# One token block goes ahead of the others, and two of four blocks take their experts by gathered rows

## The chip, the cores and the metric

The kernel runs on one core of one Trainium2 chip. A core has five engines that run at the same time, each through its own instructions in order: TensorE (PE, with its weight loads shown as PEld), VectorE (DVE), ScalarE (ACT), GpSimd (POOL) and SyncE (SP, which here only issues DMAs). Sixteen DMA engines move data between the device memory and the on-chip memory. The metric is the device time of one execution in microseconds.

## The reference, cut to what matters

512 tokens of width 2048 pass one layer. Everything is float32.

```python
def reference(...):                     # x is (1, 512, 2048)
    xn = rms_norm(h, attn_norm_gain)
    proj = xn @ w_in                    # q, k, v of 16 "fox" heads and 16 dilated heads, and forget gates
    fox_o = forgetting_attention(...)   # causal softmax attention, bias: cumulative sum of log forget gates
    dil_o = dilated_attention(...)      # causal, three (window, dilation) patterns, partial rotary
    h = h + concat(rms_norm(fox_o), rms_norm(dil_o)) @ w_out
    hn = rms_norm(h, ffn_norm_gain)
    h = h + peer(hn, ...)
    return rms_norm(h, final_norm_gain)

def peer(x, w_query, sub_keys, expert_down, expert_up):   # 16384 experts of one neuron
    q = x @ w_query                                       # 8 heads, two halves of 128
    scores = einsum('thpc,hpnc->thpn', q, sub_keys)       # 128 keys per half
    vals, idx = top_k(scores, 16)
    # the 16 largest of the 256 sums of one value of each half -> 16 experts per head, 128 per token
    hdn = gelu(einsum('ted,td->te', expert_down[experts], x))
    return einsum('te,ted->td', softmax_gates * hdn, expert_up[experts])
```

Attention is causal: a token needs the keys and values of itself and of earlier tokens only.

## The kernel before, in words

Tokens are four blocks of 128. A product of float32 numbers is made of three matmuls (`mm3`, L87 to L91): each operand is split into a high and a low part of type float32r, and high by high, high by low and low by high are summed in PSUM. A weight arrives in pieces of 128 x 1024 (512 KB). `load_split` (L75) has SP fetch the piece to `raw` (three buffers), ACT round it to `hi` (L83, two buffers) and DVE, or POOL where the caller says so, subtract to `lo` (L84, two buffers).

**Trunk.** All 512 tokens run together. The attention norm makes `xn`; `pv` makes the values (4 column groups, 8 pieces each; the weights are the moving operand, 512 columns, and one matmul serves one token block). Attention goes through 16 pairs of heads: `project` makes q and k of a pair (2 products of 2 pieces, 24 matmuls a piece, the weights stationary and all 512 tokens moving), the dilated pairs turn part of q and k by small DMAs (`rt<-xr`), and `head` makes row maxima, a transposed row of them that a DMA writes below q, weights, exponentials and the output (`o_d`, `o_f`). The tiles `qk` that hold a head's q and k have three buffers. Then come the output projection (`po`, 32 pieces), the ffn norm (`ht`), and routing: the queries (`pq`, 32 pieces, 512 tokens moving), scores, the 16 largest by DVE, and one-hot products that pick the expert numbers (L522 to L525, some on POOL).

**Dense part.** For token blocks 0 to 2 (`ND` = 384 tokens) all 16384 experts are computed and those not chosen get a gate of zero. 128 expert tiles of 128 experts: `down_tile` makes hidden values (48 matmuls, 384 tokens moving), the gates come from a table `g_d` in device memory that one-hot products fill before (L586 to L599, 12 chunks of 32 tokens, `gm`), and 32 groups of `NG` = 4 tiles are summed in PSUM per chunk of the output (`up`) and added to `yacc` on chip (L723). Ten expert tiles (`HOLD`) are computed ahead of their gates.

**Gathered block.** For block 3 (`GB`) only the chosen experts are fetched: `gather_step` (L612) issues one indirect DMA on POOL that brings one expert row of 8 KB for each of the 128 tokens (`rows`, three buffers, 1 MB), and DVE multiplies it with the token (down rows, L624) or adds it weighted (up rows, L632). 128 steps for down and 128 for up are spread over the dense part; each may start only after a named matmul of it.

**What sets the order.** The program is written straight through; a scheduler turns it into one order per engine, by place in the program and by what is ready. A tile's buffer is taken again only when its last reader is done. Each engine, and SP's queue of DMA issues too, keeps its order: an instruction that waits holds up all behind it.

Of the kernel before, what the change touches and what calls it, by code (L numbers as in the profile page):

```python
# [43 lines left out]
# pairs (i, j) of ranks that can be among the 16 largest sums, in flat order  # L44
# [5 lines left out]
def peer_block(ctx, tc, x, x_t, w_qk, w_v, w_fg, w_o, w_pq, sub_keys, down_t, down, up_t, up,  # L50
               gains, fox_bias, ffn_row, fin_row, cos_t, sin_t, dil_mask, fox_mask, out, dbg=None):
    nc = tc.nc
    dbg = dbg or {}
# [9 lines left out]
    gn = const.tile([P, 3 * NK], F32, name="gn")      # attn | fox, dil | ffn gains by feature  # L63
# [4 lines left out]
    ahead = []  # L68

    def fetch(src, pool):  # L70
        raw = pool.tile([P, 1024], F32, tag="raw", name="raw", bufs=3)
        DMA.dma_start(raw, src)
        return raw

    def load_split(src, lo_on=None, pool=None, bufs=2):  # L75
        """One piece [128, 1024] of a weight, as two float32r parts that sum to it exactly."""
        pool = pool or wts
        raw = ahead.pop(0) if ahead else fetch(src, pool)
        if isinstance(raw, tuple):
            return raw  # L80
# [12 lines left out]
    def rstd_of(ss, n, name, width=NB):  # L93
        """(ss / n + eps) ^ -1/2"""
# [11 lines left out]
    # ---------------------------------------------------------------- attention norm  # L106
    act = tc.tile_pool(name="act", bufs=1)
    act_p = act.__enter__()
    xn = [act_p.tile([P, NK, S], F32R, name=f"xn{i}") for i in range(2)]

    def split_gain(dst, k, ps, gain):
        """dst[:, k, :] (hi, lo) = gain * ps"""
        A.activation(dst[0][:, k, :], ps, AF.Copy, scale=gain)
        V.scalar_tensor_tensor(dst[1][:, k, :], ps, gain, dst[0][:, k, :].bitcast(F32), ALU.mult, ALU.subtract)

# [5 lines left out]

    wf = wts.tile([P, NK, NH], F32, tag="raw", name="wf", bufs=3)
    DMA.dma_start(wf, w_fg)
# [6 lines left out]
    with tc.tile_pool(name="xin", bufs=1, side="right") as xp:  # L130
        ones = xp.tile([P, P], F32, name="ones")
        G.memset(ones, 1.0)
        rps = bank("s", "rps")
        for t in range(NB):
            xx = xp.tile([P, D], F32, tag="x", name=f"x{t}", bufs=4)
            DMA.dma_start(xx, x[t * P:(t + 1) * P])
            junk = xp.tile([P, D], F32, name="junk", bufs=1)
            ss = xp.tile([P, 1], F32, name=f"ss{t}")
            A.activation(junk, xx, AF.Square, accum_out=ss)
            dg = diag_of(rstd_of(ss, D, f"x{t}", 1), 0, f"x{t}")  # L140
            PE.matmul(rps[:, t * P:(t + 1) * P], ones, dg, start=True, stop=True)     # rstd along the rows
        xt = []
        for q in range(4):
            xx = xp.tile([P, 4, S], F32, name=f"xt{q}")
            DMA.dma_start(xx, x_t[:, q * 4:(q + 1) * 4])
            xt.append(xx)
            if q < 2:
                ahead.append(fetch(w_v[0, q], wts))
        rb = xp.tile([P, S], F32, name="rb")
        A.copy(rb, rps)  # L150
        ahead.append(load_split(None))
        ahead.insert(0, ahead.pop())
        for k in range(NK):
            xx = xt[k // 4][:, k % 4]
            (G if k % 2 else V).tensor_tensor(xx, xx, rb, ALU.mult)
            A.activation(xn[0][:, k], xx, AF.Copy, scale=gn[:, k:k + 1])
            V.scalar_tensor_tensor(xn[1][:, k], xx, gn[:, k:k + 1], xn[0][:, k].bitcast(F32), ALU.mult, ALU.subtract)
# [4 lines left out]
    mixed = mix_p.tile([P, NB, D], F32, name="mixed")  # L162
    aug_d = dram.tile([NH, 6, 2, S], F32, name="aug_d")
    with tc.tile_pool(name="heads", bufs=1, side="right") as hp_:
# [645 lines left out]
```

## Time and profile before

| | |
|---|---|
| three runs | 3514.08, 3514.9 (median), 3518.09 us |
| profiled execution, its own time from the first to the last instruction (span) | 3513.9 us |
| PE, PEld busy | 3387.2 us (96%), 3143.6 us (89%) |
| DVE, ACT, POOL busy | 2403.6 us (68%), 1192.2 us (34%), 604.7 us (17%) |
| moved by DMA | 708.31 MB, mean 202 GB/s |

A matmul's busy time is modelled and overlaps that of the next, so PE's busy share says that it is occupied, not how fast. What a matmul costs in a stream is the length of a stretch divided by the number of matmuls in it. The profiled execution has no other time of its own than its span; it lies 1.0 us under the median of the runs.

### The profile page before, as it was taken

The numbers are of one execution on the slowest core, as the hardware profiler recorded it, in microseconds if no ns is written. First come the engines' busy times: TensorE is split into PE (matmuls) and PEld (weight loads), VectorE is DVE, ScalarE is ACT, GpSimd is POOL, SyncE is SP. The second block draws the span as 40 slices with busy tenths as digits, with TensorE's granted clock in tenths as the row PEclk, the third lists the DMA queues.
The fourth block names the chain that finished last, engine by engine and source line by source line (L and its number), as shares of the span: only waits on it lengthen the run. The fifth ranks groups of instructions, "written<-read, shape, count | busy, mean of one in ns | idle before, by whom it ended". The sixth has DMA issues, their size and how long they took to land.

```text
span 3513.9 us, 46718 instructions
## 1 busy us (share of the span) xinstructions
PE 3387.2 (96%) x18385; PEld 3143.6 (89%) x18385; DVE 2403.6 (68%) x3673; ACT 1192.2 (34%) x1655; POOL 604.7 (17%) x386
## 2 busy tenths in 40 slices
PE   6999999999998877999999999999999999999997
PEld 4887788878877766999999999999999999999997
DVE  5236654453489999677777777677777777777755
ACT  3224443342322277332323232333233232333233
POOL 2000000000154365221111211111111111111100
PEclk9999999999999899999999999999999999999999
DMA  4232222224432134877777777777777777777753
GB/s 180 90 98 65 71 76 63 74 88 141 155 97 78 37 138 166 319 277 272 282 279 280 269 281 285 279 268 283 283 279 277 274 277 288 271 273 283 289 170 108
DMA packets 197244, 708.31 MB, mean 202 GB/s; under 512 B 17888, under 2 KB 67424, under 8 KB 161184
## 3 DMA queue, kind: packets, MB, share of 16 engines
q1 hardware_dynamic: 159312, 435.43, 37.1%
q0 software_dynamic: 36864, 268.45, 19.4%
q8 instruction: 144, 2.36, 0.3%
q10 hardware_dynamic: 848, 1.44, 0.1%
q14 instruction: 76, 0.62, 0.1%
HBM read 669.08 MB, written 35.00 MB: 200 GB/s over the span
## 4 chain that ended last, share of the span: by engine, by line
PE 85%; DVE 10%; issue 2%; POOL 2%; DMA 1%; ACT 1%; ACTq 0%; SPq 0%; POOLq 0%; DVEq 0%
PE up L89 10%; PE up L91 10%; PE up L90 10%; PE dn L90 10%; PE dn L91 10%; PE dn L89 10%; PE mm L91 3%; PE mm L90 3%; PE mm L89 3%; PE po L89 2%; PE po L90 2%; PE po L91 2%; PE pv L90 1%; PE pv L91 1%; PE pv L89 1%
## 5 line engine op out<-in xcount | busy, mean ns | idle before, releaser
L83 ACT ACTIVATE hi<-raw 128x1024 fp32r<-128x1024 f32 x416 | 439.5, 1057 | 803.8 <-PE dn L91 356.8
L89 PE MATMUL dn<-hn,lo 128*128 128x384 f32 x2048 | 695.8, 340 | 4.0 <-POOL lo L84 4.0
L90 PE MATMUL dn<-hn,hi 128*128 128x384 f32 x2048 | 695.9, 340 | 0.0
L91 PE MATMUL dn<-hn,hi 128*128 128x384 f32 x2048 | 695.8, 340 | 0.0
L89 PE MATMUL up<-hn,ulo 128*128 128x384 f32 x2048 | 688.7, 336 | 3.1 <-DVE ulo L713 2.7
L91 PE MATMUL up<-hn,uhi 128*128 128x384 f32 x2048 | 688.1, 336 | 0.0
L90 PE MATMUL up<-hn,uhi 128*128 128x384 f32 x2048 | 688.1, 336 | 0.0
L84 DVE TENSOR_TENSOR lo<-raw,hi 128x1024 fp32r<-128x1024 f32 x366 | 447.8, 1224 | 282.6 <-ACT hi L83 282.3
L712 ACT ACTIVATE uhi<-uraw 128x1024 fp32r<-128x1024 f32 x256 | 271.7, 1062 | 631.9 <-PE up L91 615.8
L632 DVE SCALAR_TENSOR_TENSOR yg<-rows,coef,yg 128x2048 f32<-128x2048 f32 x127 | 298.5, 2350 | 224.4 <-DMA rows<-in_up,gidx 224.4
L624 DVE SCALAR_TENSOR_TENSOR rows<-rows,hng 128x2048 f32<-128x2048 f32 x128 | 293.2, 2290 | 223.2 <-DMA rows<-in_down,gidx 223.1
L89 PEld LDWEIGHTS dn<-hn,lo 128*128 128x128 f32 x2048 | 386.1, 189 | 5.2 <-POOL lo L84 4.3
L89 PEld LDWEIGHTS up<-hn,ulo 128*128 128x128 f32 x2048 | 385.0, 188 | 4.3 <-PE up L91 3.6
L91 PEld LDWEIGHTS dn<-hn,hi 128*128 128x128 f32 x2048 | 386.0, 188 | 0.4
L90 PEld LDWEIGHTS dn<-hn,hi 128*128 128x128 f32 x2048 | 385.7, 188 | 0.5
L90 PEld LDWEIGHTS up<-hn,uhi 128*128 128x128 f32 x2048 | 385.0, 188 | 0.0
L91 PEld LDWEIGHTS up<-hn,uhi 128*128 128x128 f32 x2048 | 385.0, 188 | 0.0
L713 DVE TENSOR_TENSOR ulo<-uraw,uhi 128x1024 fp32r<-128x1024 f32 x256 | 312.1, 1219 | 10.6 <-ACT uhi L712 10.1
L620 POOL DMA_INDIRECT rows<-in_down,gidx x128 | 174.8, 1366 | 776.6 <-PE up L91 640.6
L723 DVE TENSOR_TENSOR yacc<-yacc,up 128x384 f32<-128x384 f32 x496 | 261.3, 548 | 56.4 <-PE up L91 55.9
L620 POOL DMA_INDIRECT rows<-in_up,gidx x128 | 160.6, 1254 | 794.1 <-PE up L91 612.2
L90 PE MATMUL mm<-xn,hi 128*128 128x512 f32 x512 | 203.8, 398 | 0.0
(235 smaller groups left out, 4509.0 us busy)
## 6 DMA issues: line engine op xcount, KB each, us to landing
raw<-in_down_t SPq DMA_DIRECT2D x256, 512.0 KB
uraw<-in_up_t SPq DMA_DIRECT2D x256, 512.0 KB
raw<-in_w_qk SPq DMA_DIRECT2D x64, 512.0 KB
g_d<-stg SPq DMA_DIRECT2D x12, 2048.0 KB
gt<-g_d SPq DMA_DIRECT2D x32, 768.0 KB
raw<-in_w_v SPq DMA_DIRECT2D x32, 512.0 KB
raw<-in_w_o SPq DMA_DIRECT2D x32, 512.0 KB
raw<-in_w_pq SPq DMA_DIRECT2D x32, 512.0 KB
```

Source lines behind the costliest of these rows:

```text
L83: A.activation(hi, raw, AF.Copy)
L84: (lo_on or V).tensor_tensor(lo, raw, hi.bitcast(F32), ALU.subtract)
L89: PE.matmul(ps, a[1], b[0], start=first, stop=False)
L90: PE.matmul(ps, a[0], b[1], start=False, stop=False)
L91: return PE.matmul(ps, a[0], b[0], start=False, stop=last)
L620: ld = G.indirect_dma_start(out=rows, out_offset=None, in_=down if n < HK else up, in_offset=bass.IndirectOffsetOnAxis(ap=gidx[:, j:j + 1] ...
L624: V.scalar_tensor_tensor(rows, rows, 1.0, hng, ALU.mult, ALU.mult, accum_out=udot[:, j:j + 1])
L632: V.scalar_tensor_tensor(yg[0], rows, coef[:, j:j + 1], yg[0], ALU.mult, ALU.add)
L712: A.activation(uh, raw, AF.Copy)
L713: V.tensor_tensor(ul, raw, uh.bitcast(F32), ALU.subtract)
L723: V.tensor_tensor(yacc[:, c], yacc[:, c], ps[:, :ND], ALU.add)
```

## The change

Block 0 goes through norm, values, attention, output projection, ffn norm and routing alone. Then blocks 1 to 3 (384 tokens, `NL` = 3) do the same, reading block 0's keys from device memory (`k_d`), and meanwhile block 0's experts are gathered: 128 of its 256 steps are written into the second trunk (2 per two pieces of the values, 4 per pair of heads, 1 per piece of the output projection), with two buffers `rows`. Blocks 2 and 3 (256 tokens) run dense, block 1 is gathered; the other 128 steps of block 0 and the 256 of block 1 are spread evenly over all but the last group of the dense part. Each weight of the trunk is fetched and split twice, once with 128 and once with 384 tokens; `lo` alternates between POOL and DVE there. `qk` has two buffers instead of three. The sum in PSUM runs over 8 expert tiles, so there are 16 groups and the moving operand of the dense part has 256 columns. The gate table has 8 chunks, 12 expert tiles are computed ahead.

```diff
-ND = 384
-NDB = ND // P
-GB = NB - 1
-HOLD = 10
+NL = NB - 1
+NDB = 2
+ND = NDB * P
+D0 = NL - NDB
+HOLD = 12
+NG = 8
...
+    def alternate():
+        turn[0] += 1
+        return G if turn[0] % 2 else V
...
+        def step(after, rows_pool, bufs):
+            n = state["n"]
+            if n >= 2 * HK:
+                return False
+            state["n"] += 1
+            rows = rows_pool.tile([P, D], F32, tag="rows", name=f"rows{nm}{n}", bufs=bufs)
+            j = n % HK
+            ld = G.indirect_dma_start(out=rows, out_offset=None, in_=down if n < HK else up,
+                                      in_offset=bass.IndirectOffsetOnAxis(ap=gidx[:, j:j + 1], axis=0))
+            tc.add_manual_dep(ld.ins, after.ins.name, PACE, reason="pace")
...
+    def gather0(n):
+        for _ in range(n):
+            step0(last[0], rows0_p, 2)
...
+                hi, lo = load_split(w_v[g, pc], alternate())
...
+                if b0 and pc % 2:
+                    gather0(2)
...
+            def new_qk(hd):
+                qk = ap.tile([P, 4, S], F32R, tag="qk", name=f"qk{b0}{hd}", bufs=2)
+                if b0:
+                    DMA.dma_start(qk[:HD, 0, :P].bitcast(F32), k_d[hd, :HD])
+                    DMA.dma_start(qk[:, 2, :P].bitcast(F32), k_d[hd])
+                return qk
...
+                if b0:
+                    gather0(4)
...
+                hi, lo = load_split(w_o[g, pc], alternate())
...
+                if b0:
+                    gather0(1)
...
+    trunk_norm(0, 1, xn)
+    forget_gates(0, 1, xn)
+    values(0, 1, xn)
+    mix_r = attention(0, 1, xn, mixed0, xn_cm)
+        h, hss = out_rows(0, 1, mixed0, mix_r, mx, rp, ...)
+        ffn_norm(0, 1, h, hss, hn, chain_bank, rp, hng_here)
+            route(0, 1, hn, top0, ex0, chain_bank, rr, lambda src, hp: load_split(src, alternate()), 0)
...
+    trunk_norm(1, NL, xn)
+    forget_gates(1, NL, xn)
+    values(1, NL, xn)
+    mix_r = attention(1, NL, xn, mixed, xn_cm)
+    h, hss = out_rows(1, NL, mixed, mix_r, mx, rp, ...)
+    ffn_norm(1, NL, h, hss, hn, aux, rp, hng_store)
+        route(1, NL, hn, top, ex, aux, rr,
+              lambda src, hp: load_split(src, G, rr, 4) if hp else load_split(src), 0)
...
-                for _ in range(1 + (dc == 0)):
-                    gather_step(mm)
+                want = -(-left * (g * NK + c + 1) // chunks)
+                while done < min(want, left):
+                    gather(mm)
+                    done += 1
```

## Rows read from the trace of the kernel before

**Rows 1.** The page: busy time of engines, then the chain that ended last.

```profile
PE 3387.2 (96%) x18385; PEld 3143.6 (89%) x18385; DVE 2403.6 (68%) x3673; ACT 1192.2 (34%) x1655; POOL 604.7 (17%) x386
PE 85%; DVE 10%; issue 2%; POOL 2%; DMA 1%; ACT 1%; ACTq 0%; SPq 0%; POOLq 0%; DVEq 0%
```

**Rows 2.** Stages: start:end length, busy us (count) by engine, clock, DMA share, GB/s.

```profile
0.00:25.00 25.00, 3.30 (x9) 2.15 (x9) 7.49 (x13) 14.00 (x16) 9.00 (x16) 1.00 0.92 371
25.00:229.00 204.00, 195.80 (x816) 151.81 (x817) 73.82 (x74) 50.36 (x58) 9.06 (x7) 0.98 0.31 96
229.00:760.00 531.00, 527.93 (x2679) 423.93 (x2677) 292.16 (x679) 223.04 (x400) 1.02 (x1) 1.00 0.23 70
760.00:932.00 172.00, 171.97 (x749) 139.31 (x748) 67.15 (x85) 46.70 (x72) 1.57 (x2) 1.00 0.43 133
932.00:961.00 29.00, 26.33 (x176) 23.50 (x176) 16.70 (x29) 14.80 (x23) 5.12 (x5) 1.00 0.58 214
961.00:1222.00 261.00, 231.98 (x1045) 192.34 (x1043) 232.43 (x1009) 57.17 (x72) 124.91 (x54) 0.94 0.23 74
1222.00:1402.00 180.00, 136.78 (x928) 119.62 (x929) 174.18 (x99) 134.46 (x236) 106.11 (x39) 0.96 0.37 146
1402.00:3464.00 2062.00, 2061.61 (x11801) 2061.09 (x11800) 1509.71 (x1638) 634.36 (x751) 345.58 (x261) 1.00 0.76 273
3464.00:3513.90 49.90, 31.54 (x193) 29.82 (x191) 29.96 (x51) 17.32 (x32) 2.36 (x3) 0.89 0.25 93
```

**Rows 3.** The same columns, a stretch of the values alone, 512 columns moving.

```profile
100.00:150.00 50.00, 50.00 (x217) 40.54 (x216) 12.42 (x11) 10.73 (x11) 0.00 (x0) 1.00 0.30 92
```

**Rows 4.** The chain in order of time (start, us, what): two dilated pairs.

```profile
336.21 2.23 PE o_d L273 x20
...
368.65 2.23 PE o_d L273 x20
```

**Rows 5.** Groups by line and form: the split of a weight piece.

```profile
L84 DVE TENSOR_TENSOR lo<-raw,hi 128x1024 fp32r<-128x1024 f32 x366 | 447.8, 1224 | 282.6 <-ACT hi L83 282.3
L83 ACT ACTIVATE hi<-raw 128x1024 fp32r<-128x1024 f32 x416 | 439.5, 1057 | 803.8 <-PE dn L91 356.8 <-PE po L91 116.8 <-PE mm L91 111.0
...
L84 POOL TENSOR_TENSOR lo<-raw,hi 128x1024 fp32r<-128x1024 f32 x50 | 126.9, 2544 | 88.6 <-ACT hi L83 88.6
```

**Rows 6.** DMA queues from 1402 to 3464: packets, MB, share of 16 engines.

```profile
q1 hardware_dynamic: 122121, 292.17, 42.4%
q0 software_dynamic: 36864, 268.45, 33.1%
```

**Rows 7.** Groups of VectorE from 1402 to 3464, by line and form.

```profile
L713 DVE TENSOR_TENSOR ulo<-uraw,uhi 128x1024 fp32r<-128x1024 f32 x251 | 306.0, 1219 | 10.6 <-ACT uhi L712 10.1
L632 DVE SCALAR_TENSOR_TENSOR yg<-rows,coef,yg 128x2048 f32<-128x2048 f32 x127 | 298.5, 2350 | 224.4 <-DMA rows<-in_up,gidx 224.4
L624 DVE SCALAR_TENSOR_TENSOR rows<-rows,hng 128x2048 f32<-128x2048 f32 x128 | 293.2, 2290 | 223.2 <-DMA rows<-in_down,gidx 223.1
...
L723 DVE TENSOR_TENSOR yacc<-yacc,up 128x384 f32<-128x384 f32 x483 | 254.1, 548 | 46.6 <-PE up L91 46.1
L701 DVE TENSOR_TENSOR hold<-hold,gt 128x384 f32<-128x384 f32 x128 | 71.2, 561 | 37.6 <-DMA gt<-g_d 26.1 <-ACT hold L550 11.5
L705 DVE TENSOR_TENSOR hn<-hold,hn 128x384 fp32r<-128x384 f32 x128 | 65.5, 551 | 1.1 <-ACT hn L704 1.1
```

**Rows 8.** Groups of VectorE from 229 to 760: the same operation at 256 columns.

```profile
L266 DVE TENSOR_TENSOR w_d<-w_d,dmask 128x256 f32<-128x256 f32 x16 | 6.8, 423 | 0.0
```

**Rows 9.** The tile `rows` from 1402 to 3464: from issue to landing.

```profile
DMA to landing us min/median/max: 6.1/9.4/12.5
```

**Rows 10.** Groups by line and form: the one-hot tables of the gates.

```profile
L587 DVE TENSOR_TENSOR o<-iota_e,i1t 128x1024 f32<-128x1024 f32 x48 | 110.9, 2311 | 0.8 <-ACT i1t L573 0.8
...
L586 DVE TENSOR_TENSOR o<-iota_e,i2t 128x1024 f32<-128x1024 f32 x48 | 69.0, 1438 | 0.3 <-ACT i2t L573 0.3
```

More of the change, by code (lines that the diff above doesn't have):

```diff
@@ L128, in fox_bank @@
         return bank(("s", "s", "s", "o")[n % 4], name)
[L130 to L157, printed above, removed]
@@ L276, in head @@
+                for i in range(nb):
+                    for kb in range(b0 + i + 1):
+                        pt, qs = pts[kb]
+                        o = q0 + i * P - qs
+                        last[0] = PE.matmul(op[:, i], pt[:, o:o + P], v_all[:, kb, hd], start=kb == 0, stop=kb == b0 + i)
+                rd = st[:, nb:].unsqueeze(2)
                 V.reciprocal(rd, op[:, :, HD:HD + 1])
-                V.tensor_tensor(mixed[:, :, ocol:ocol + HD], op[:, :, :HD], rd.broadcast_to([P, NB, HD]), ALU.mult)
@@ L388, in peer_block @@
-    h = hpool.tile([P, NB, D], F32, name="h")
-    hss = hpool.tile([P, NB, 4], F32, name="hss")
-    with tc.tile_pool(name="res", bufs=1, side="right") as rp:
+                    head(qks[z], HD + 4, mask, P, 2 * c + z, (2 * c + z) * HD, f"f{b0}{2 * c + z}")
+            squares(0)
+        mix_r = {}
+        for half in range(2):
+            ss = small.tile([P, NB], F32, name=f"gss{b0}{half}")
+            V.tensor_reduce(ss[:, :nb], mss[:, half, :, 0:2], AX.X, ALU.add)
+            mix_r[half] = small.tile([P, NB], F32, name=f"mixr{b0}{half}")
+            V.tensor_copy(mix_r[half][:, :nb], rstd_of(ss[:, :nb], W, f"g{b0}{half}", nb)[:, :nb])
@@ L441, in peer_block, with ffn_norm @@
-    with tc.tile_pool(name="rows", bufs=1, side="right") as rp:
+                DMA.dma_start(h_d[(b0 + t) * P:(b0 + t + 1) * P, gs], h[:, t, gs])
+        return h, hss
+    def ffn_norm(b0, nb, h, hss, hn, new_bank, rp, hng_out):
+        hsum = small.tile([P, NB], F32, name=f"hsum{b0}")
+        hdiag = []
+        for t in range(nb):
+            V.tensor_reduce(hsum[:, t:t + 1], hss[:, t], AX.X, ALU.add)
+            r = rstd_of(hsum[:, t:t + 1], D, f"h{b0}{t}", 1)
+            hdiag.append(diag_of(r, 0, f"h{b0}{t}"))
+            if t == 0:
+                rfirst = small.tile([P, 1], F32, name=f"rfirst{b0}")
+                V.tensor_copy(rfirst, r[:, 0:1])
+        for k in range(NK):
+            ps = new_bank(f"ht{b0}{k}")
+            for t in range(nb):
+                PE.matmul(ps[:, t * P:(t + 1) * P], h[:, t, k * P:(k + 1) * P], hdiag[t], start=True, stop=True)
+            psr = ps[:, :nb * P].rearrange("p (b t) -> p b t", b=nb)
+            gain = gn[:, 2 * NK + k:2 * NK + k + 1]
+            A.activation(hn[0][:, :, k], psr, AF.Copy, scale=gain)
+            V.scalar_tensor_tensor(hn[1][:, :, k], psr, gain, hn[0][:, :, k].bitcast(F32), ALU.mult, ALU.subtract)
@@ L450, in peer_block, with route @@
[L450 to L458 removed]
+            hng_out(q, cs, fr, h[:, 0, cs], rfirst)
+    def route(b0, nb, hn, top, ex, new_bank, rp, split, gathers):
+        n = nb * P
@@ L691, in peer_block @@
             down_tile(e, G)
-        NG = 4
+        groups = NE1 // NG
+        left = 4 * HK - state0["n"]
+        chunks = (groups - 1) * NK
+        done = 0
         pslot = 0
-        for g in range(NE1 // NG):
-            gt = xp.tile([P, NGC, NG, GC], F32, name="gt", bufs=1)
+        for g in range(groups):
+            gt = xp.tile([P, NGC, NG, GC], F32, tag="gt", name="gt", bufs=1)
             DMA.dma_start(gt, g_d[:, :, g * NG:(g + 1) * NG, :].rearrange("c p e t -> p c e t"))
@@ L724, in peer_block @@
-                if dc % 2:
-                    e = HOLD + g * NG + dc // 2
+                ps = aux("up")
+                for j in range(NG):
+                    mm = mm3(ps[:, :ND], (uh[:, j], ul[:, j]), pp[j], j == 0, j == NG - 1)
+                if g == 0:
+                    V.tensor_copy(yacc[:, c], ps[:, :ND])
+                else:
+                    V.tensor_tensor(yacc[:, c], yacc[:, c], ps[:, :ND], ALU.add)
+                if c % 2:
+                    e = HOLD + g * NG + c // 2
```

606 lines of the change are left out of this document (313 added, 293 removed).

## The prediction, written before the change was run

> **What bounds the kernel now.** I read the page first: PE is occupied for 96% of the span and makes 85% of the chain that ended last [rows 1], so a product is on the path nearly everywhere. Then the windows by stage [rows 2]. The reader is to see two programs one after the other. Up to 1402 us (trunk, routing, gates) the DMA engines are idle for most of the time, with a share of 0.23 to 0.58 after the first 25 us. From 1402 to 3464 PE never stops, DVE is busy for 1510 of 2062 us (73%) and DMA for 0.76 at 273 GB/s. So in the dense part PE is the bound, and the two next resources have a quarter left each. The change narrows what PE does there and adds to what the other two do.
>
> Matmul prices. 2062 us for 11,801 matmuls is 0.1747 us at 384 columns [rows 2]; 50 us for 217 is 0.2304 at 512 [rows 3]; 128 columns cost 0.0557. On that line 256 columns cost 0.119 and 128 cost 0.063. But 20 matmuls of 66 columns, each with its own weights, take 2.23 us [rows 4], 0.1115 each: below some 240 columns the weight load sets the pace. For 256 I take 0.119 (ends 0.1115 and 0.1747), for 128 I take 0.1115.
>
> The Trainium skill ("TensorE: Matmul & The Clock Gate", Back-to-back issue gap) gives about 81 ns for a 128-column matmul with its weight load, sustained. The trace is slower, 0.1115 us in float32. By the page the estimate below would be 2304 x 0.0305 = 70 us less, 3623; I go by the row.
>
> **Block 0 alone, all of it new time before the second trunk.** The wide-moving products (values and output projection, 512 weight columns moving) need as many matmuls as before, one block's share here. q, k and the routing queries (96 pieces of 24 matmuls, 2304) run once with 128 and once with 384 columns: 2304 x (0.1115 + 0.1747) = 659 us for 531.
>
> With one block a piece gives PE little work, and the split becomes the limit. `lo` alternates POOL 2.544 and DVE 1.224, `hi` takes 1.057 [rows 5], and `hi` and `lo` have two buffers, so every second piece goes through a slot that ACT, POOL and PE hold in turn. For a piece with 6 matmuls of 512 columns: (1.057 + 2.544 + 1.382) / 2 = 2.49 us; with 24 of 128 columns: (1.057 + 2.544 + 2.676) / 2 = 3.14 us. The transfer of 0.524 MB takes 1.4 us at the 371 GB/s of the first stage [rows 2], so DMA is not first.
> - norm: 25 us as now [rows 2].
> - values: 32 x 2.49 = 80.
> - attention: 64 x 3.14 = 201. A pair takes 32.4 us now [rows 4], of which 96 x 0.2304 = 22.1 is projection and 10.3 is heads; at one block of queries I take 2.5 a pair, so 15 a pair, 240. Ends: 201 (heads hidden) and 16 x (12.6 + 10.3) = 366, where the heads' chain of small DMAs stays as long as it is and two buffers `qk` instead of three hold back the next pair.
> - output projection: 32 x 2.49 and some 10 of transposes, 90. ffn norm: 15 of the 29 now [rows 2].
> - routing: 32 x 3.14 = 100, and 12 for the last head's chain.
>
> Sum: 562 us. Storing block 0's keys adds SP issues that nothing waits for.
>
> **Blocks 1 to 3, with 128 gathers beside.** A gather takes 6.1 us to land at best, 9.4 at the median under the dense part's load [rows 9], and 2.3 us of DVE [rows 7]. With two buffers that is (6.1 + 2.3) / 2 = 4.2 us each at least, 5.9 at most. What is queued behind: POOL is in order, a gather that waits for a buffer holds up the next `lo` on POOL, and PE waits for that. So gathers aren't free where they come faster than every 4.2 us.
> - seam between the trunks: 20 (norm again, xn after block 0's routing).
> - values: PE 576 x 0.2304 = 133, gathers 32 x 4.2 = 134; I take 150 (ends 134 and 187).
> - attention: 531 now, less 1536 x 0.2304 = 354, leaves 177 for heads and gaps; three blocks of queries, but all keys: 150. With 1536 x 0.1747 = 268 that is 418. DVE: (292 - 78 of `lo`) x 0.85 + 39 + 64 x 2.32 = 369 us of these 418, and 4 gathers a pair take at least 17 us of POOL's order. I add 47: 465 (ends 418 and 540). Fetching block 0's keys (64 loads) lies under the projections of the pair; uncovered it would be some 2 us a head.
> - output projection: 10, then PE 133 against gathers 134: 155. ffn norm: 25.
> - routing: DVE 232 now [rows 2], 0.8 of it, 190. Gates: DVE bound now (174 of 180); 32 steps of 1.438 + 2.311 us [rows 10] and 2: 122. The 12 tiles ahead (576 x 0.119 = 69 us of PE) hide there, as ten do now.
>
> Sum: 1127. So the dense part starts at 1689 instead of 1402: 287 later.
>
> **Dense part, 256 columns, 15 groups with 384 gathers.**
> - PE: (116 + 128) tiles x 48 x 0.119 = 1394 us, against 2062. PE gives back some 670 us if nothing else is late.
> - DMA: a gather is 268.45 / 256 = 1.049 MB; 384 are 402.7 MB, at 268.45 / (0.331 x 2062) = 393 GB/s [rows 6] 1024 us. Weights 236 x 1.049 and the gate table 15.7 MB are 263 MB, at 292.17 / (0.424 x 2062) = 334 GB/s [rows 6] 788 us. Sum 1812 us with all engines busy all the time; by the mean of the stage, 273 / 0.76 = 359 GB/s, 1855.
> - DVE: gathers 384 x 2.32 and the readouts 16: 907; `lo` and `ulo` 472 x 1.22 = 576 [rows 5, 7]; `yacc` 240 x 0.423 = 102 and the two steps of `hold` 240 x 0.42 = 101 (548 to 561 ns at 384 columns [rows 7], 423 at 256 [rows 8]). Sum 1686. Eight tiles a sum save DVE 170 us of `yacc`; PE doesn't wait for it now, so this pays only as room.
>
> So DMA is next, DVE just behind it, and both run through three buffers in order. The highest DMA share of a whole stage is 0.92, in the first 25 us [rows 2]. I take 0.94: 1812 / 0.94 = 1928. Ends: 1686 (DVE alone) and the stalled case below. The last group and the end: 384 x 0.119 = 46 and some 30: 75, against 50 from 3464 now.
>
> Total: 562 + 1127 + 1928 + 75 = 3692 against the profiled 3513.9: the front is 287 longer, the rest 109 shorter. The span lies 1 us under the median of the runs: 3693.
>
> **Rivals.**
> - A, faster: the DMA engines reach in the dense part what they reach at the start, 371 / 0.92 = 403 GB/s. For it: that row is long transfers without other work, and gathers already move at 393. Against it: the weight stream moves at 334 beside them. Then 666 MB take 1652 us, DVE's 1686 decide, and the time is 562 + 1127 + 1686 + 75 = 3450. It turns to a gain where the rate passes 666 / (3513.9 - 1689 - 75) = 381 GB/s. The Trainium skill ("DMA: Bandwidth & Descriptors", Where 436 GB/s comes from) says that loads from device memory end at some 358 GB/s a core. By it, as an estimate, the stage takes 1860 us and A falls out, the total being 3624; the 371 of the first 25 us is above it, so A stands.
> - B, slower still: DVE stalls at its gathers as now, 224.4 + 223.2 us for 256 [rows 7], 1.75 us each. Now PE's lead covers this. With 384 gathers it is 672 us on top of 1686: 2358, and a total of 4122. For it: the wait is on landing, and landing gets slower as the load rises. Against it: where DVE has spare time, as now, a wait costs nothing and so says little of a full DVE.
> - C, the front is at PE's floor: splits and gathers hide. Block 0: 25 + 44 + 172 + 40 + 54 + 10 + 98 = 443; blocks 1 to 3: 20 + 134 + 418 + 143 + 25 + 312 = 1052. With the dense part of the forecast, 443 + 1052 + 1928 + 75 = 3498, a gain of 0.5%. For it: PE's pitch is held through the whole trunk now [rows 2]. Against it: the slot worked out from [rows 5] needs no bad luck.
> - D: the 128 gathers in the trunk stall it by as much as they save later (POOL's order). At 5.9 us each in place of 4.2, 128 x 1.7 = 218: 3910.
>
> PE's granted clock is 1.00, the level of 2.4 GHz, where PE runs on, and 0.94 to 0.96 in routing and gates, where it pauses and some of the time is at 1.2 GHz [rows 2]; at 70% occupancy in the dense part this would cost PE, which has room.
>
> **How the numbers follow.** Forecast 0.50 (its own range 3580 to 3830), A 0.16, B 0.10, C 0.10, D 0.14. A measurement of this kernel tells 0.2%, 7 us, from no change. Faster: A, and some 0.06 of C, which ends near the line: 0.22. Same: 0.03. Slower: 0.75. The range leaves out the lower half of A, and B: 3450 to 3920.
>
> **What would show it.** Right: block 0's routing ends near 560 us, the gates near 1690; there PE has pauses before pieces whose `lo` is POOL's; from then DMA has a share above 0.9, PE waits for `lo`, `ulo` or `hi`, and PE makes some 117 matmuls in 20 us (11,712 in 2003) where 168 would fit. Wrong in the front: block 0 done by 450. Wrong in the dense part: it takes under 1830 us with DMA at 380 GB/s or more (A), or DVE waits for `rows` by 500 us or more (B).

## The result: a fifth slower, and later than predicted

The changed kernel takes 4216.7 us (median of four runs, 4209.3 to 4227.4) against 3514.9: a ratio of 1.1995, 95% interval 1.1974 to 1.2015. The prediction was 3693, range 3450 to 3920. The direction was right; the loss was 702 us where 178 was forecast, outside the range. The profiled execution has a span of 4225.5 us, 533 more than the sum of 3692.

The page after (busy time of the engines, then the chain that ended last):

```profile
PE 3377.8 (80%) x20558; PEld 3161.7 (75%) x20558; DVE 2891.5 (68%) x4230; ACT 1348.8 (32%) x2065; POOL 1298.1 (31%) x784
DMA 27%; issue 14%; DVE 12%; PE 6%; POOL 2%; ACT 0%; DVEq 0%; POOLq 0%; ACTq 0%
```

PE was 85% of the chain before [rows 1] and is 6% now; the first place is taken by DMA, and the lines of the page behind it are the landings of `rows`. The stages of the kernel after, in the columns of [rows 2]:

```profile
17.00:122.00 105.00, 67.53 (x247) 47.22 (x248) 38.84 (x47) 46.31 (x59) 43.28 (x25) 0.89 0.57 192
122.00:520.00 398.00, 383.71 (x1734) 370.54 (x1733) 111.25 (x336) 123.76 (x288) 75.30 (x32) 0.50 0.28 95
520.00:612.00 92.00, 63.79 (x203) 44.06 (x202) 35.27 (x49) 41.35 (x58) 39.33 (x19) 0.83 0.62 202
...
640.00:806.00 166.00, 147.60 (x664) 143.74 (x664) 82.24 (x352) 36.12 (x56) 38.82 (x18) 0.50 0.29 101
...
830.00:996.00 166.00, 138.63 (x553) 106.47 (x552) 103.55 (x86) 38.12 (x43) 78.54 (x43) 0.92 0.73 272
996.00:1640.00 644.00, 518.91 (x2565) 475.94 (x2564) 397.04 (x692) 207.79 (x405) 186.82 (x101) 0.81 0.48 172
1640.00:1820.00 180.00, 139.64 (x553) 109.66 (x551) 114.89 (x109) 42.15 (x64) 67.62 (x47) 0.91 0.79 290
...
1850.00:2060.00 210.00, 181.55 (x1054) 177.56 (x1052) 184.71 (x802) 58.25 (x75) 116.35 (x48) 0.93 0.28 98
2060.00:2190.00 130.00, 95.05 (x692) 87.40 (x693) 119.67 (x65) 94.51 (x166) 77.89 (x29) 0.95 0.38 154
2190.00:4175.00 1985.00, 1539.09 (x11610) 1505.70 (x11608) 1609.88 (x1511) 599.34 (x750) 544.07 (x393) 0.89 0.91 345
```

Beside the forecast (us):

| part | forecast | after | difference |
|---|---|---|---|
| block 0: values, attention, output projection | 80, 240, 90 | 105, 398, 92 | |
| block 0: ffn norm and routing (from 612) | 15, 112 | 6, 188 | |
| block 0 alone, with its norm | 562 | 806 | +244 |
| blocks 1 to 3: seam, values, attention, output projection | 20, 150, 465, 155 | 24, 166, 644, 180 | |
| blocks 1 to 3: ffn norm, routing, gates | 25, 190, 122 | 30, 210, 130 | |
| blocks 1 to 3, to the end of the gates | 1127 | 1384 | +257 |
| dense part and end | 2003 | 2035 | +32 |

Two misses of about 250 us lie in the two trunks. The dense part took what was forecast, but the experiments show another cause than the one given.

**What the first trunk shows.** A stretch of q and k in block 0, and the group it belongs to (by line and form, 122 to 520):

```profile
156.50:169.50 13.00, 13.00 (x63) 13.00 (x63) 3.27 (x10) 3.51 (x7) 2.35 (x1) 0.50 0.24 86
L90 PE MATMUL mm<-xn,hi 128*128 128x128 f32 x512 | 212.9, 416 | 0.0
```

PE is occupied for all of the 13.00 us and its granted clock is 0.50, the level of 1.2 GHz. From start to start a matmul takes 0.213 us (the count of 63 takes in two that the edges cut); the forecast had 0.1115, from rows at a clock of 1.00 [rows 4]. The first matmuls of the same stream ran at that price. The first row has the columns of [rows 2]; the others are single matmuls in order of time (start, us, what), of which those between are left out:

```profile
121.90:123.60 1.70, 1.70 (x17) 1.70 (x17) 1.23 (x1) 0.22 (x1) 0.00 (x0) 1.00 0.53 190
```

```profile
122.05 0.27 PE L88 MATMUL mm<-xn,lo 128*128 128x128 f32 x1
...
123.61 0.27 PE L90 MATMUL mm<-xn,hi 128*128 128x128 f32 x1
...
124.10 0.41 PE L90 MATMUL mm<-xn,hi 128*128 128x128 f32 x1
...
125.80 0.41 PE L89 MATMUL mm<-xn,hi 128*128 128x128 f32 x1
```

From 122.05 to 123.61 there are 14 steps of 0.111 us at a clock of 1.00, from 124.10 to 125.80 there are 8 of 0.213 at 0.50. So the price was right for its level, and the level was not kept: PE was occupied without a gap when the clock fell, and it stayed at 0.50 to the end of the stream. Of the stages, the two with the 128-column products (122 to 520 and 640 to 806) have a clock of 0.50, all others 0.77 or more.

**What the dense part shows.** VectorE's groups by line and form, 2190 to 4175, and the waits of all engines in the same stretch (engine, line, what ended the wait, us, times, longest):

```profile
L137 DVE SCALAR_TENSOR_TENSOR yga<-rowsa,coefa,yga 128x2048 f32<-128x2048 f32 x127 | 298.5, 2350 | 103.0 <-DMA rowsa<-in_up,gidx 102.6
L137 DVE SCALAR_TENSOR_TENSOR ygb<-rowsb,coefb,ygb 128x2048 f32<-128x2048 f32 x127 | 298.4, 2350 | 102.6 <-DMA rowsb<-in_up,gidx 102.4
L806 DVE TENSOR_TENSOR ulo<-uraw,uhi 128x1024 fp32r<-128x1024 f32 x245 | 297.0, 1220 | 6.5 <-ACT uhi L805 5.6
L129 DVE SCALAR_TENSOR_TENSOR rowsb<-rowsb,hng 128x2048 f32<-128x2048 f32 x128 | 293.0, 2290 | 108.1 <-DMA rowsb<-in_down,gidx 107.7
L83 DVE TENSOR_TENSOR lo<-raw,hi 128x1024 fp32r<-128x1024 f32 x232 | 281.5, 1220 | 0.0
L813 DVE TENSOR_TENSOR yacc<-yacc,up 128x256 f32<-128x256 f32 x227 | 90.7, 416 | 19.7 <-PE up L90 19.2
```

```profile
POOL rowsb L125 <- PE up L90: 447.5, 71, 22.4
ACT uhi L805 <- PE up L90: 410.3, 169, 11.4
PEld up L88 <- DVE ulo L806: 292.1, 86, 16.5
PE up L88 <- DVE ulo L806: 287.3, 84, 16.3
```

The landing of the gathers of block 1 in this stretch (tile `rowsb`):

```profile
DMA to landing us min/median/max: 5.7/9.2/14.1
```

VectorE is busy for 1610 of 1985 us and stands 314 us at rows not landed, 0.82 us for each of 384 gathers (1.75 in [rows 7]). PE waits for VectorE's `ulo`, and GpSimd waits 447 us, at the gathers of block 1 alone, for a matmul of `up` before it may issue the next one: the matmul that the gather is bound to.

### The profile page after: what moved, and what is told of

It reads as the page before. It is cut to its first block, busy times and chain, and to the rows that moved or that the text cites. A ratio compares the mean times of both kernels' runs of the same rounds, so it can differ in the third digit from the quotient of the medians.

```text
span 4225.5 us, 54212 instructions
## 1 busy us (share of the span) xinstructions
PE 3377.8 (80%) x20558; PEld 3161.7 (75%) x20558; DVE 2891.5 (68%) x4230; ACT 1348.8 (32%) x2065; POOL 1298.1 (31%) x784
## 3 DMA queue, kind: packets, MB, share of 16 engines
q10 hardware_dynamic: 1376, 1.97, 0.1%
## 4 chain that ended last, share of the span: by engine, by line
DMA 27%; issue 14%; DVE 12%; PE 6%; POOL 2%; ACT 0%; DVEq 0%; POOLq 0%; ACTq 0%
DMA rowsb<-in_up,gidx 8%; DMA rowsb<-in_down,gidx 8%; DMA rowsa<-in_up,gidx 8%; DMA rowsa<-in_down,gidx 3%; DVE ygb L137 2%; DVE yga L137 1%; PE up L88 1%; DVE rowsb L129 1%; PE up L90 1%; PE up L89 1%; DVE ulo L806 1%; DVE o L693 1%; DVE lo L83 1%; DVE o L692 1%; POOL rowsb L125 1%
## 5 line engine op out<-in xcount | busy, mean ns | idle before, releaser
L83 POOL TENSOR_TENSOR lo<-raw,hi 128x1024 fp32r<-128x1024 f32 x198 | 492.6, 2491 | 889.7 <-ACT hi L82 888.2
L88 PE MATMUL dn<-hn,lo 128*128 128x256 f32 x2048 | 614.2, 300 | 165.4 <-DVE lo L83 153.5
L89 PE MATMUL dn<-hn,hi 128*128 128x256 f32 x2048 | 604.1, 295 | 0.0
L90 PE MATMUL dn<-hn,hi 128*128 128x256 f32 x2048 | 603.1, 295 | 0.0
L129 DVE SCALAR_TENSOR_TENSOR rowsa<-rowsa,hng 128x2048 f32<-128x2048 f32 x128 | 328.5, 2568 | 183.5 <-DMA rowsa<-in_down,gidx 183.1
L88 PE MATMUL up<-spare,ulo 128*128 128x256 f32 x1024 | 311.1, 304 | 172.2 <-DVE ulo L806 172.1
L88 PE MATMUL mm<-xn,lo 128*128 128x128 f32 (+1 forms) x1024 | 403.0, 394 | 9.8 <-POOL lo L83 3.6
L88 PE MATMUL up<-hn,ulo 128*128 128x256 f32 x1024 | 308.5, 301 | 117.5 <-DVE ulo L806 115.2
L89 PE MATMUL mm<-xn,hi 128*128 128x128 f32 (+1 forms) x1024 | 400.6, 391 | 0.0
L90 PE MATMUL mm<-xn,hi 128*128 128x128 f32 (+1 forms) x1024 | 400.1, 391 | 0.0
L137 DVE SCALAR_TENSOR_TENSOR yga<-rowsa,coefa,yga 128x2048 f32<-128x2048 f32 x127 | 298.5, 2350 | 103.0 <-DMA rowsa<-in_up,gidx 102.6
L137 DVE SCALAR_TENSOR_TENSOR ygb<-rowsb,coefb,ygb 128x2048 f32<-128x2048 f32 x127 | 298.4, 2350 | 102.6 <-DMA rowsb<-in_up,gidx 102.4
```

The source lines that it names most:

```text
L88: PE.matmul(ps, a[1], b[0], start=first, stop=False)
L89: PE.matmul(ps, a[0], b[1], start=False, stop=False)
L90: return PE.matmul(ps, a[0], b[0], start=False, stop=last)
L129: V.scalar_tensor_tensor(rows, rows, 1.0, hng, ALU.mult, ALU.mult, accum_out=udot[:, j:j + 1])
L137: V.scalar_tensor_tensor(state["y"], rows, coef[:, j:j + 1], state["y"], ALU.mult, ALU.add)
```

## The experiments

All times are of one core; a version that was run once has no interval.

### The price of block 0's narrow products

`e1_twice`, the changed kernel with the tokens of block 0 streamed twice through q, k and the routing queries; half of each result is unused.

```diff
+ mv = [z[:, k] for z in xn]
+ wide = n
+ if nb == 1:
+     mv = [z.unsqueeze(1).broadcast_to([P, 2, P]) for z in mv]
+     wide = 2 * n
- last[0] = mm3(ps[:, :n], (hi[:, sl], lo[:, sl]), (xn[0][:, k], xn[1][:, k]), ...
+ last[0] = mm3(ps[:, :wide], (hi[:, sl], lo[:, sl]), mv, ...
...                                      # the same for the routing queries
```

> The changed kernel, in which block 0's q, k and routing queries stream their 128 tokens twice (256 columns, the second half is not read). Theory, the clock: a 128-column stream with a weight load per matmul leaves PE at 1.2 GHz although it never pauses, 0.213 us a matmul; with 256 columns the clock goes to 2.4 GHz and a matmul takes 0.119. 2304 x 0.094 = 216 us less: about 4000 us, block 0 routed near 590 us instead of 806, granted clock 0.9 or more in its attention. Rival, the split of the weights (the slot of ACT, POOL and PE) or the heads' chain sets the pace: doubling the columns changes nothing or costs up to 100 us, 4210 to 4320. Rival, the clock is low for pauses of PE: 256 columns then take 0.213 as well, 4217.

4076.9 us (4064.6 to 4084.8), ratio 1.1588 [1.1559, 1.1616]: 140 less than after, with twice the columns in those 2304 matmuls. A stretch of it, and its block-0 attention:

```profile
122.00:128.00 6.00, 5.94 (x48) 5.74 (x48) 1.23 (x1) 1.35 (x3) 1.71 (x1) 1.00 0.48 175
122.00:421.00 299.00, 245.03 (x1735) 226.95 (x1735) 134.48 (x338) 123.50 (x288) 76.29 (x32) 0.91 0.38 127
```

The 48 matmuls of two pieces fit into the 6.00 us at a clock of 1.00, 0.120 from start to start (46 steps from 122.15 to 127.66 us). What PE does before 122 us is nearly the same in both runs (clock 0.84 to 0.96 there), so the columns of the stream made the difference. Block 0's attention falls from 398 to 299 and the second trunk starts 146 earlier. The theory holds in kind and not in size: the price alone would give 2304 x (0.213 - 0.120) = 214. Behind faster projections the heads and other pauses show, and over the whole attention the clock is 0.91: 299 less 1536 x 0.120 = 184 leaves 115, 7.2 a pair, where 398 less 1536 x 0.213 = 327 leaves 71, 4.4 a pair.

`e6_before_qk2`, the kernel before with two buffers `qk` instead of three, alone.

```diff
- qks = [ap.tile([P, 4, S], F32R, tag="qk", name=f"qkd{2 * c + z}", bufs=3) for z in range(2)]
+ qks = [ap.tile([P, 4, S], F32R, tag="qk", name=f"qkd{2 * c + z}", bufs=2) for z in range(2)]
```

> The kernel before with two buffers qk instead of three, nothing else. If two buffers hold back the next pair of heads, its attention (229 to 760 us) grows by 4 us a pair or more, 60 to 150 us in all: 3575 to 3665. If the projections of the next pair, whose sums wait in PSUM, cover it: 3515 to 3525.

3519.2 us against 3514.6, ratio 1.0015 [1.0005, 1.0024]: 5 us with all four blocks, as the second of the two cases has it. The changed kernel was not run with three.

### The price of 128 gathers in the second trunk

Versions of the changed kernel, which take apart what a gather is: an issue on GpSimd, a transfer of 1 MB, and 2.3 us of VectorE.

`e2_no_gathers` leaves the 128 steps out (block 0 lacks its down products). `e2_no_dve` issues and lands them, VectorE leaves them unused.

```diff
  def gather0(n):
-     for _ in range(n):
-         step0(last[0], rows0_p, 2)
+     return                              # e2_no_gathers
...
-     V.scalar_tensor_tensor(rows, rows, 1.0, hng, ALU.mult, ALU.mult, accum_out=udot[:, j:j + 1])
+     if use:                             # e2_no_dve: False in the second trunk
+         V.scalar_tensor_tensor(rows, rows, 1.0, hng, ALU.mult, ALU.mult, accum_out=udot[:, j:j + 1])
```

> The changed kernel without the 128 gathers of block 0 in the second trunk (its down products are left out and a constant stands for them; the dense part keeps its 384 gathers). Theory: VectorE, in order, stands at a gather that has not landed, the heads' work waits behind it, PE pauses and its clock falls: without them the attention of blocks 1 to 3 takes some 450 us instead of 644, values 145 instead of 166, output projection 150 instead of 180; about 4000 us. Rival, two buffers qk and the fetch of block 0's keys hold the pairs apart: attention stays above 600 us, total above 4150.

> The changed kernel in which the 128 gathers of the second trunk are issued and land as before, but VectorE's product on each is left out. Theory, VectorE waits for landings and holds up the heads: as good as without the gathers, attention near 450 to 480 us, total 4000 to 4040. Rival, GpSimd's order (a gather that waits for a buffer holds up lo): attention stays near 640. Half of each: some 550.

`e9_quarter` is the second with an eighth of the bytes (other rows are fetched, nothing uses them); `e11_work_only` has VectorE's products on data that is already there, without transfers.

```diff
+ src = src.rearrange("e (a d) -> (e a) d", d=256)                  # e9_quarter
- ld = G.indirect_dma_start(out=rows, in_=src, ...)
+ ld = G.indirect_dma_start(out=rows[:, :256], in_=src, ...)
...
- V.scalar_tensor_tensor(rows, rows, 1.0, hng, ...)
+ V.scalar_tensor_tensor(rows, hng, 1.0, hng, ...)                  # e11_work_only, no DMA (second trunk)
```

> The run in which VectorE leaves the 128 gathers of the second trunk unused, with one more thing taken away: each of them fetches rows of 256 numbers (1 KB) instead of 2048 (8 KB), so they are issued as often and move an eighth. There the second values began at 801 us and the gates at 1925; without any gathers the gates began at 1791. Theory (the bytes: 1 MB gathers delay the weight pieces and the heads' small transfers): the gates begin by 1830, total under 3995. Rival (the issue on GpSimd, its place in GpSimd's order and its two buffers): the gates stay at 1900 or later, total over 4055. Between: both, by the share.

> The changed kernel without the 128 transfers of the gathers in the second trunk, but with VectorE's 128 products (2.3 us each) kept, on data that is already there. With neither the gates begin at 1791 us, with the transfers alone at 1925, with both at 2063. Theory (VectorE's 294 us of work by themselves lengthen the heads' chain, beside what the transfers do): the gates begin at 1900 to 1940, total 4060 to 4100. Rival (VectorE's part is the standing at rows that have not landed, 63 us in the second attention; the work lies in its pauses): by 1850, total under 4010.

| second trunk has | total, us | gates start | above none |
|---|---|---|---|
| no gathers (`e2_no_gathers`) | 3950.9 | 1791 | |
| issues and 1/8 of the bytes (`e9_quarter`) | 3972.0 | 1806 | 15 |
| issues and all bytes (`e2_no_dve`) | 4084.6 | 1925 | 134 |
| VectorE's work alone (`e11_work_only`) | 4069.4 | 1914 | 123 |
| all (after) | 4216.7 | 2063 | 272 |

Step by step the 272 us are 15 for the issues with an eighth of the bytes, 119 more with all bytes, and 138 more when VectorE uses the rows. The 15 are no more than the 18 us between the executions of after, so they are not told from nothing. Without gathers the attention comes to 483, and the rival, that two buffers `qk` and the fetch of keys hold it above 600, falls. In `e2_no_dve` it takes 574, near the 550 named for half of each. In `e9_quarter` the theory of the bytes holds (1806 and 3972.0).

`e11_work_only` came out as its theory said (1914 and 4069.4), but not by the heads' chain. With no transfer to wait for, its products run early, all from 623 to 1143 us:

```profile
L131 DVE SCALAR_TENSOR_TENSOR rowsa<-hng x128: 2216/2279/4508, 623.2 to 1140.7; 128x2048 f32<-128x2048 f32 x128
```

The second values begin at 859 us instead of 802, so 57 of the 123 us lie in block 0's routing, and the attention is only 31 longer. What VectorE's work costs in the place where after has it, this run does not show. The second attention in these four runs, one fence each in the order of the table:

```profile
950.00:1433.00 483.00, 453.34 (x2600) 418.19 (x2599) 240.70 (x556) 208.06 (x406) 81.78 (x34) 0.94 0.26 86
```

```profile
956.00:1446.00 490.00, 456.94 (x2593) 421.19 (x2592) 242.94 (x554) 207.96 (x405) 160.46 (x104) 0.93 0.32 103
```

```profile
965.00:1539.00 574.00, 492.06 (x2551) 449.47 (x2550) 236.68 (x552) 203.87 (x402) 143.78 (x100) 0.84 0.54 194
```

```profile
1041.00:1555.00 514.00, 463.64 (x2597) 426.66 (x2596) 297.72 (x602) 209.90 (x407) 92.48 (x34) 0.92 0.25 81
```

The same 1536 projections run in all of them, and the stretch is 483 to 574 us long; after has 644, and there the granted clock is 0.81 instead of 0.94. The clock is a part of the cost: PE is busy with these projections for 295 us without gathers and for 329 in after. DMA's mean share is only 0.54 in the run with all bytes: a free share does not say that a small transfer on which a head waits comes through as fast. From the second values to the output projection, PE's waits for the row of maxima below q are 27 us in `e2_no_dve` and 3 without gathers; how much of the 119 each transfer carries (that row, the turned parts `rt`, the weight pieces) was not told apart.

`e5_no_dve_lo_v` is `e2_no_dve` with every `lo` of the values, q, k and output projection of blocks 1 to 3 on VectorE instead of half of them on GpSimd, behind the gathers.

```diff
- hi, lo = load_split(w_v[g, pc], alternate())
+ hi, lo = load_split(w_v[g, pc], V if b0 else alternate())
```

> As the run without VectorE's products on the trunk's gathers (which are issued and land), and lo of blocks 1 to 3 in values, attention and output projection is made on VectorE alone instead of alternating with GpSimd. That run's second trunk from its first value to its last output projection took 801 to 1680 us, and without gathers 802 to 1556; 64 of these 124 us lie in the attention before its last output (574 to 483). Theory, GpSimd's order: a gather that waits for one of two buffers holds up lo, so with lo elsewhere the stretch comes to 780 us or less, total near 3990. Rival, the gathers' bytes delay the heads' small DMAs and the weights: the stretch stays at 860 to 890, total 4070 to 4100.

4102.8 against 4084.6: nothing gained. By itself this doesn't clear GpSimd's order, since 64 more pieces of `lo` (some 78 us, estimated from 1.22 each [rows 5]) now load VectorE. PE's waits in after, from the second values to the output projection (802 to 1818), speak against it:

```profile
PE po L89 <- DVE lo L83: 31.9, 12, 5.0
PE pv L89 <- DVE lo L83: 25.2, 12, 3.7
PE po L89 <- POOL lo L83: 6.7, 1, 6.7
```

PE waits 61 us for VectorE's `lo` (under 1 without gathers) and 10 for GpSimd's (4 without gathers, 13 in `e2_no_dve`). SP's queue, in which the heads' small transfers stand too, waits 204 us for GpSimd's `lo` (265 without gathers) and 220 for VectorE's (82). The pieces that come late come from VectorE, where a product of a gather stands ahead of the split.

`e4_defer` writes each product in the second trunk one place after its issue, before the next issue; the gathers go two to a place (per head, per two pieces).

```diff
  def gather0(n):
+     while pend:
+         pend.pop(0)()
      for _ in range(n):
-         step0(last[0], rows0_p, 2)
+         step0(last[0], rows0_p, 2, pend)
```

> The changed kernel with VectorE's product of a trunk gather put one place later: two gathers are issued at a place (per head, per two pieces), and used at the next place, when they have landed. Same work. Theory, VectorE stood at gathers that had not landed: attention of blocks 1 to 3 falls from 644 to some 500 us, total some 4050 to 4080. Rival, VectorE's or GpSimd's load itself or the buffers qk are the price: no change beyond 30 us.

4178.1 us (4169.5 to 4183.8), ratio 1.1879 [1.1857, 1.1901]: 39 less, between the theory and its rival; the attention takes 611. VectorE's products of the second trunk in after, then in `e4_defer`:

```profile
L129 DVE SCALAR_TENSOR_TENSOR rowsa<-rowsa,hng 128x2048 f32<-128x2048 f32 x128 | 328.5, 2568 | 183.5 <-DMA rowsa<-in_down,gidx 183.1
L130 DVE SCALAR_TENSOR_TENSOR rowsa<-rowsa,hng 128x2048 f32<-128x2048 f32 x128 | 336.7, 2630 | 148.7 <-DMA rowsa<-in_down,gidx 148.5
```

The edit took away only 35 of the 183 us that VectorE stands at rows, and the time fell by as much. How the 138 us divide between standing and work stays open.

`e10_twice_defer` joins `e1_twice` and `e4_defer`; its diff is the two above.

> Two edits of earlier runs together: block 0's stationary products stream the tokens twice (140 us less by itself), and each product of a gather in the second trunk is written one place later (39 us less by itself). Theory (two separate costs, one in each trunk): they add up, 4216.7 - 140 - 39 = 4038, within 12. Rival (what is saved in one place is lost in the other, since the dense part sets the pace from both): less than 150 together, over 4066.

4046.0 us (4033.2 to 4059.0), ratio 1.1523 [1.1486, 1.156], against 4038 for a plain sum: they add up within the 12 us named.

### What bounds the dense part

`e7_dense_narrow`: VectorE works on 64 of 2048 columns of each gather in the dense part (products incomplete). `e8_dense_less_dma`: every third gather there is not fetched, VectorE works on other data (experts left out).

```diff
+ w = D if bufs == 2 else 64                                        # e7_dense_narrow
- V.scalar_tensor_tensor(rows, rows, 1.0, hng, ...)
+ V.scalar_tensor_tensor(rows[:, :w], rows[:, :w], 1.0, hng[:, :w], ...)
...                                                                 # the same for the up rows
+ skip = bufs == 3 and n % 3 == 1                                   # e8_dense_less_dma
+ if not skip:
      ld = G.indirect_dma_start(out=rows, ...)
...
- V.scalar_tensor_tensor(rows, rows, 1.0, hng, ...)
+ V.scalar_tensor_tensor(rows, hng if skip else rows, 1.0, hng, ...)
...
```

> The changed kernel; in the dense part VectorE works on 64 of the 2048 columns of each of the 384 gathers, which are fetched whole. VectorE falls from some 1640 to 800 us there. Theory of the prediction, DMA bounds the dense part at 1812 us of work with a share of 0.91: from 2190 to 4175 us (1985) it falls little, to 1830 to 1930, at a share of 0.95 or more. Rival, VectorE bounds it or stalls in order at landings: it falls to what DMA allows at once, 1812, and PE's clock returns to 1.00.

> The changed kernel; in the dense part every third of the 384 gathers is not fetched, and VectorE does its product on resident numbers instead, so it has the same work. DMA has 134 MB less, 341 us of 1812. Theory, DMA bounds: the dense part falls from 1985 to VectorE's own 1640 to 1690 and some waiting, 1720 to 1800. Rival, VectorE's in-order work and waits bound it: it stays above 1880.

3948.3 and 4139.8 us. From the first to the last matmul of `up` (the same stretch is 1993 us in after), `e7_dense_narrow`, then `e8_dense_less_dma`:

```profile
2227.00:3933.00 1706.00, 1460.65 (x11738) 1432.31 (x11739) 846.17 (x1532) 583.14 (x753) 504.79 (x386) 0.95 0.99 399
```

```profile
2221.00:4125.00 1904.00, 1539.90 (x11738) 1512.02 (x11738) 1616.81 (x1531) 600.62 (x753) 382.32 (x259) 0.90 0.78 288
```

With VectorE out of the way the same transfers take 1706 us at 399 GB/s, less than the 1812 that both expectations counted as DMA's work; with a third of the gathers gone DMA falls to 0.78 and the stage stays above 1900, as the rival said. DMA was not the bound.

`e12_all_late` is `e10_twice_defer` with the products in the dense part written two gathers late; `e13_early` is `e10_twice_defer` with each gather there bound to the matmul two places earlier; `e14_early_late` has both.

```diff
  def gather(after):
+     while len(late) > 1:                                          # e12_all_late
+         late.pop(0)()
-     return step0(after, rows_p, 3) or step1(after, rows_p, 3)
+     return step0(after, rows_p, 3, late) or step1(after, rows_p, 3, late)
...
+ seen.append(mm)                                                   # e13_early
- gather(mm)
+ gather(seen[max(0, len(seen) - 3)])
```

> The run with both edits (4046.0) and one more: in the dense part each gather's product is written two places after its issue, about 10 us later. There VectorE works 1610 us and stands 314 us at rows not yet landed. Theory (these waits are part of the bound, beside VectorE's work): most of the 314 goes, the dense part shrinks from 1990 to between 1700 and 1800, total 3760 to 3860; the floor is the 1706 us of the run in which VectorE works narrow and the DMA engines are at a share of 1.00. Rival (the waits are only the place where VectorE's slack shows; transfers or VectorE's work among the splits decide): the waits move to other instructions and the total stays over 3990.

> The run with both edits in the trunks (4046.0; dense part 1993 us), with one more: in the dense part a gather is bound to the matmul two places (about 15 us) earlier than its own, its product stays where it is. Theory (a closed loop sets the pace: GpSimd may issue only after the matmul of the place, 521 us of waits for it in the last run, the rows land some 9 us later, VectorE's product stands at them, the split behind the product is late, and with it the next matmul): the waits at rows fall under 150 us of 300 and the dense part to 1750 to 1870, total 3800 to 3920. Rival (VectorE's 1634 us and the DMA engines' share of 0.91 bound it together, whatever the issues wait for): over 1950 in the dense part, total over 4000.

> The last run (4010.0: products two gathers late), with the gathers bound to the matmul two places earlier as well. Theory of the loop: as much or more than the earlier binding alone, 3780 to 3900. Rival (VectorE and the DMA engines bound it together): 3990 or more.

| run | total, us | ratio [interval] | first to last `up` | VectorE busy | stands at rows | rest |
|---|---|---|---|---|---|---|
| after | 4216.7 | 1.1995 [1.1974, 1.2015] | 1993 | 1627 | 318 | 48 |
| `e10_twice_defer` | 4046.0 | 1.1523 [1.1486, 1.156] | 1992 | 1627 | 321 | 44 |
| `e12_all_late` | 4010.0 | 1.14 [1.1379, 1.1422] | 1959 | 1624 | 273 | 62 |
| `e8_dense_less_dma` | 4139.8 | one run | 1904 | 1617 | 226 | 61 |
| `e13_early` | 3919.8 | 1.1142 [1.1107, 1.1176] | 1881 | 1622 | 180 | 79 |
| `e14_early_late` | 3868.8 | 1.1011 [1.0993, 1.1029] | 1822 | 1619 | 140 | 63 |

The rest, all other idle time of VectorE, is only 44 to 79 us in all six: where the stage gets shorter, it is the standing that shrinks. The later product alone did little (its rival, over 3990, was the one that held, though its reason, that the waits only show slack, fell with the next two runs); the earlier binding took 111 us from the stage, both 170. In `e13_early` two of the three bounds that the theory named were missed: 1881 where 1870 was the end, 180 where 150 was. The stage, VectorE's groups and GpSimd's waits in `e14_early_late`:

```profile
2032.00:3854.00 1822.00, 1510.22 (x11738) 1483.53 (x11739) 1619.47 (x1531) 601.89 (x753) 517.44 (x386) 0.92 0.96 374
```

```profile
L138 DVE SCALAR_TENSOR_TENSOR yga<-rowsa,coefa,yga 128x2048 f32<-128x2048 f32 x127 | 298.2, 2348 | 47.2 <-DMA rowsa<-in_up,gidx 47.0
L138 DVE SCALAR_TENSOR_TENSOR ygb<-rowsb,coefb,ygb 128x2048 f32<-128x2048 f32 x127 | 298.1, 2347 | 48.6 <-DMA rowsb<-in_up,gidx 48.1
L130 DVE SCALAR_TENSOR_TENSOR rowsb<-rowsb,hng 128x2048 f32<-128x2048 f32 x128 | 292.7, 2293 | 43.0 <-DMA rowsb<-in_down,gidx 42.8
```

```profile
POOL rowsa L125 <- DVE yga L138: 212.1, 62, 10.4
POOL rowsb L125 <- DVE ygb L138: 202.8, 62, 9.0
POOL rowsb L125 <- DVE rowsb L130: 201.4, 57, 10.4
```

The wait for the matmul of `up` is no longer among GpSimd's largest (78 us at block 1's gathers, 447 in after); GpSimd now waits for VectorE to free a buffer. The same operations cost the same (2.35 and 2.29 us); the waits more than halved. So a loop set the pace: matmul, issue, landing (median 9.2 us), product, the split behind it, the next matmul. PE's 1510 us fit into the stage with room, and yet PE took part in the bound, because each gather was tied to it. In the kernel before, with the same binding, PE was occupied for 2061.6 of 2062 us [rows 2], so there was nothing to lose. What is left, 140 us of standing and a DMA share of 0.96, is close to the 1706 us of `e7_dense_narrow`.

No version beat the kernel before: the best, 3868.8, is 355 us behind it, and the distance from there to 1706 us in the dense part is 116.

## Why the prediction was wrong, step by step

- **"PE's granted clock is 1.00, the level of 2.4 GHz, where PE runs on" failed**, and with it "for 128 I take 0.1115". At a clock of 1.00 the narrow products did take 0.111, but the stream ran at 0.50 and 0.213, with PE occupied. In the sum a piece went by the slot of ACT, POOL and PE, 3.14 us; at 24 x 0.213 = 5.11 PE alone set the pace, and 96 x 1.97 = 189 of the 244 us that block 0 missed are this price. `e1_twice` gives 146 back. The two levels were named only for stretches in which PE pauses.
- The Trainium skill ("TensorE: Matmul & The Clock Gate", What's actually happening) describes 1.2 GHz as the state of an idle or cold array that activity releases. Here PE was occupied without a gap and stayed at it; the measurement decides. The 81 ns that the prediction took from the same page of the Trainium skill were met at neither level (0.111 and 0.213 us). The 70 us that it worked out from them left out the slot: by that figure of the Trainium skill they would be, as an estimate, 96 x (3.14 - 2.77) = 35.
- **"attention ... 2.5 a pair" for the heads failed in size**: 4.4 a pair show in after, 7.2 in `e1_twice` behind faster projections, between the 2.5 taken and the 10.3 kept as an end. So even there block 0's attention takes 299, not 240.
- **Block 0's values**, 105 for 80, were not tested. From 17 to 122 us PE waits 25 us for POOL's `lo` and 10 for ACT's `hi`, so the slot was there; why a piece took longer than its 2.49 us stays open.
- **The gathers in the second trunk were under-priced.** They entered the sum as 17 + 47 + 12 = 76 us and cost 272. The step that failed is "POOL is in order, a gather that waits for a buffer holds up the next `lo` on POOL, and PE waits for that" as the price: PE waits 10 us for POOL's `lo` there. Left out were the transfers' effect on other transfers (119) and VectorE's use of the rows on the path of heads and splits (138), with a clock that fell as PE paused more. VectorE's 369 us "of these 418" was counted as share, not as order.
- **The second attention without gathers** takes 483 where 418 was taken, above even the 465 that should have held them. These 65 and the 196 us of the gathers (272 less 76) are, within 4 us, the 257 that the second trunk missed.
- **Rival D had the place (the 128 gathers stall the trunk) and the wrong mechanism**: it charged GpSimd's order, 218 us.
- **The dense part: right number, wrong cause; that it came out is luck.** 1928 was DMA work at 359 to 393 GB/s and a share of 0.94. The 117 matmuls in 20 us came true (11,610 in 1985 us), the share was 0.91. But `e7_dense_narrow` moves the same at 399 GB/s and a share of 0.99. Rates worked out from a queue's share in an unsaturated stage [rows 6] were a lower bound. The Trainium skill ("DMA: Bandwidth & Descriptors", Where 436 GB/s comes from) gets its 358 GB/s by halving 716 between two cores. Here one core ran and passed it with 399; no run shows two.
- **Rival A had the rate right** (403 GB/s forecast) and was wrong that VectorE's work alone would then decide: **rival B's mechanism was there**, at 0.82 us a gather instead of 1.75. VectorE's work was sized at 1686 and is 1627. A cause was named for B (landing slower under load) that the runs don't bear out: landing stayed at a median of 9.2 us (9.4 in [rows 9]), and `e8_dense_less_dma`, with less load, stands 0.88 us at each fetched gather (226 / 256). Binding the issue earlier took 141 of 321 us of standing away.
- **Rival C** (the front at PE's floor, 3498) fell with both trunks.
- **Right:** VectorE's steps at 256 columns (416 ns for 423), PE no longer first, two buffers `qk` (5 us in the kernel before), the gates (130 for 122), routing of blocks 1 to 3 (210 for 190).
- **Eight tiles a sum were to pay "only as room".** VectorE's work then lay on the path, so what they save there counts: with four, some 240 more steps of 0.416 us, 100 us, as an estimate from the rows above; no run has four.

## What to carry to other kernels

A matmul price holds at the granted clock of the rows it comes from: when a change makes products narrower, take the price at both levels and carry both through the sum, even where PE will never pause. Work put into the pauses of a chain of small dependent steps costs through order and through other transfers, not by its share of an engine: here an engine at 50% and DMA engines at 26% turned 128 gathers into 272 us. And a pacing dependence that is free while one engine is the bound becomes part of a loop as soon as that engine isn't; move it earlier before anything else.

## What the hardware showed unexpectedly

- 128-column float32r matmuls, each with its own weights, began at 0.111 us and a clock of 1.00, fell to 0.50 without a pause of PE, and went on at 0.213 us. The same matmuls with 256 columns, half of them useless: 0.120 us at 1.00.
- The DMA engines of the one core moved 399 GB/s over 1706 us in a mix of weight stream and gathered 8 KB rows, share 0.99 (one run).
